# FF1 of a decoder layer: weight sums formed by accumulating transfers instead of VectorE

## The chip, the cores and the metric

The kernel runs on one core of a Trainium2 chip. The metric is the time of one execution on the device, in microseconds (us); less is better. A profile is one execution with the profiler on, with the busy time and the waits of each engine: TensorE (PE: matmuls; PEld: its weight loads), VectorE (DVE), ScalarE (ACT), GpSimd (POOL) and SyncE (SP), and the 16 DMA engines. Only SP and POOL issue transfers in this kernel.

## The reference

One decoder layer on 512 tokens with 2048 features, in float32. The first half (attention beside a recurrence) is not touched. The second half is

```python
h = rms_norm(x, g_pre_mlp[l]) * (1.0 + sc2) + sh2
f = jnp.square(jax.nn.relu(h @ w_ff1[l])) @ w_ff2[l]
x = x + gt2 * rms_norm(f, g_post_mlp[l])
```

with `w_ff1` of 2048 x 8192 and `w_ff2` of 8192 x 2048. FF1 is `h @ w_ff1` with its squared ReLU, FF2 the product with `w_ff2`.

## The kernel before

**Two parts for one number.** Each float32 operand of a product is split into `hi` (rounded to float32r by a ScalarE Copy) and `lo` (the rest, a VectorE subtract). A product is three matmuls, hi x hi, hi x lo and lo x hi (`mmh`, L1131 to L1133).

**Seven products for eight.** FF1 multiplies 2 x 2 blocks with seven products in place of eight: sums of weight blocks times sums of token blocks. A unit of output is q, 0 to 31: 256 rows of the hidden layer, as two halves of 128. The weights of q lie in HBM as four groups g, each `wff1[q, g]` of 128 x 1024: four blocks R0, R1, R2, R3 of 256 columns, in this order (both halves of the features, both halves of the output). The products need R1, R2, R3 as they are and four sums:

- S0 = R0 + R1, S1 = R0 + R2 (one VectorE add of 512 columns, L1290, with R0 read twice),
- S2 = S0 + R2 (L1293),
- S3 = S2 + R3 (L1294).

**The list of groups, `GR`.** It holds 16 entries of kind "a" (two blocks of two groups, no sums; their products are kept in `P1`), then 48 of kind "b" (q below 12: five products, R1 and the sums are split) and 80 of kind "c" (seven products, everything is split). A product of a group takes two steps of 128 rows, three matmuls each, so a "b" group has 5 x 2 x 3 = 30 matmuls of 128 x 256 and a "c" group 7 x 2 x 3 = 42.

**One turn of the loop, for group s:** `group(s)` issues the matmuls; `raw_load(s + 3)` issues the load of a later group into the tile `fr` (three of them; 512 KB by one transfer on SP's queue); `open_banks(s + 2)` clears PSUM; `forms(s + 2)` makes the sums in the tile `fs` (two of them), and splits blocks and sums into `fh` and `fl` (two of each, 1792 columns: three blocks, then four sums). It does so in two steps: Copy (L1289) and subtract (L1295) of the blocks, Copy (L1296) and subtract (L1297) of the sums. After the last group of q, `pair_end` combines the seven products on VectorE in `X`, applies ReLU and square on ScalarE into `ust` (two of them), and POOL stores the result to `ud` in HBM, 512 KB for a "c" q, 128 and 256 KB for a "b" q. FF2 reads it back from there.

**What sets the order.** The code is written in this order, and the framework then orders each engine's instructions by a plan of its own in which an instruction may pass earlier ones that are not ready; that order is fixed when the kernel is built. On the chip each engine and each DMA queue runs its list in order and waits at an instruction whose inputs or buffer are not ready. The tiles of `fp` (left side of SBUF) live for all of FF1. Those of `fp2` (right side: `fs`, `X`, `ust`) take the room of `h` (`hst`, `Hf`), so they come into being two groups ahead of the first "b" group, when `t_forms` has read the last of `h`.

Of the kernel before, what the change touches and what calls it, by code (L numbers as in the profile page):

```python
# [7 lines left out]
F32 = mybir.dt.float32  # L8
F32R = mybir.dt.float32r
AF = mybir.ActivationFunctionType  # L10
OP = mybir.AluOpType
# [119 lines left out]
def hybrid_block_kernel(ctx: ExitStack, tc: tile.TileContext, xT, c, vec, wada, wst, win, wv0, wv1,  # L131
                        w1, w2, pe, wrg, wout, wff1, wff2, xN, out):
    nc = tc.nc
    V, A, T, G = nc.vector, nc.scalar, nc.tensor, nc.gpsimd

    def f(ap):
        return ap.bitcast(F32)
# [10 lines left out]
    def ps(tag):  # L148
        return psum.tile([128, 512], F32, name="ps_" + tag, tag=tag, bufs=NB[tag])
# [250 lines left out]
    for j in range(4):  # L400
# [3 lines left out]
        p = ps("pj")  # L404
# [736 lines left out]
    def relu2(q, m, x, sgn, t_):  # L1141
        A.activation(x, x, AF.Relu, scale=sgn)
        A.activation(t_, x, AF.Square)

    def alpha_end(q, p, pool, tg, nb):
        A.activation(P1[q], p[:, T1], AF.Copy)
        x = pool.tile([128, 256], F32, name="ax", tag=tg, bufs=nb)
        u = pool.tile([128, 256], F32, name="au", tag=tg, bufs=nb)
        V.tensor_add(x, p[:, T2], P1[q])
        relu2(q, 0, x, 1.0, u)  # L1150
        G.dma_start(ud[q][:, 0, T1], u)
# [59 lines left out]
    fp = fst.enter_context(tc.tile_pool(name="fp", bufs=1, reuse_waits="tile"))  # L1211
    P1 = {q: fp.tile([128, 256], F32, name=f"p1_{q}") for q in range(NA1 + NA2)}
    for q in range(NA1):
        alpha_end(q, pf[q], fp, "ax", 2)
    THx = fp.tile([128, 2, 8, 256], F32R, name="thx")
    TLt = fp.tile([128, 4, D], F32R, name="tlt")
    TH = {5: lambda j: AH[:, j, T2], 7: lambda j: AL[:, j, T2],
# [7 lines left out]
    def hq(tok, kh, hh, of=Hf):  # L1225
        c0 = 1024 * kh + 512 * hh
        return of[:, 2 * tok:2 * tok + 2, c0:c0 + 512]

    def t_forms():
        for hh in range(2):  # L1230
            h11, h12, h21, h22 = hq(0, 0, hh), hq(1, 0, hh), hq(0, 1, hh), hq(1, 1, hh)
            ks_ = slice(4 * hh, 4 * hh + 4)

            def part(v, lo, hi):
                lo = lo.rearrange("p c (k t) -> p c k t", k=4)
                v = v.rearrange("p c (k t) -> p c k t", k=4)
                hi = hi.rearrange("p k (c t) -> p c k t", c=2)
                A.activation(hi, v, AF.Copy)
                V.tensor_sub(lo, v, f(hi))
            V.tensor_sub(h11, h11, h12)  # L1240
            yield
            V.tensor_sub(h12, h22, h12)
            yield
            V.scalar_tensor_tensor(h22, h11, -1.0, h22, op0=OP.mult, op1=OP.subtract)
            yield
            V.scalar_tensor_tensor(h21, h21, -1.0, h22, op0=OP.mult, op1=OP.subtract)
            yield
            for v, a_, hi in ((h11, (0, 0), AH[:, ks_, T2]), (h12, (1, 0), AL[:, ks_, T2]),
                              (h22, (1, 1), THx[:, 0, ks_]), (h21, (0, 1), THx[:, 1, ks_])):
                part(v, hq(*a_, hh, TLt), hi)  # L1250
                yield

    GR = []
# [4 lines left out]
    RAW, FM, FP2 = {}, {}, {}  # L1258
    gst = ExitStack()

    def raw_load(s):
        if s >= len(GR):
            return
        kind, q, g = GR[s]
        R = fp.tile([128, 1024], F32, name="fr", tag="fr", bufs=3)
        if kind == "a":
            nc.sync.dma_start(R.rearrange("p (a b) -> p a b", a=2),
                              wff1[q, g:g + 2, :, 512:].rearrange("a p b -> p a b"))
        else:
            nc.sync.dma_start(R, wff1[q, g])  # L1270
        RAW[s] = R

    def forms(s):
        if s >= len(GR):
            return
        kind = GR[s][0]
        R = RAW.pop(s)
        hi = fp.tile([128, 1792], F32R, name="fh", tag="fh", bufs=2)
        lo = fp.tile([128, 1792], F32R, name="fl", tag="fl", bufs=2)
        FM[s] = hi, lo  # L1280
        if kind == "a":
            for c_ in (0, 512):
                sl = slice(c_, c_ + 512)
                A.activation(hi[:, sl], R[:, sl], AF.Copy)
                V.tensor_sub(lo[:, sl], R[:, sl], f(hi[:, sl]))
            return
        Sm = FP2["p"].tile([128, 1024], F32, name="fs", tag="fs", bufs=2)
        n = 256 if kind == "b" else 768
        A.activation(hi[:, :n], R[:, 256:256 + n], AF.Copy)  # L1289
        V.tensor_add(Sm[:, :512].rearrange("p (a b) -> p a b", a=2),  # L1290
                     R[:, 256:768].rearrange("p (a b) -> p a b", a=2),
                     R[:, None, :256].to_broadcast([128, 2, 256]))
        V.tensor_add(Sm[:, 512:768], Sm[:, :256], R[:, 512:768])  # L1293
        V.tensor_add(Sm[:, 768:], Sm[:, 512:768], R[:, 768:])  # L1294
        V.tensor_sub(lo[:, :n], R[:, 256:256 + n], f(hi[:, :n]))  # L1295
        A.activation(hi[:, 768:], Sm, AF.Copy)  # L1296
        V.tensor_sub(lo[:, 768:], Sm, f(hi[:, 768:]))  # L1297

    banks = ["S", "T", "S", "T", "pj", "pj", "pj", "O"]
    nb = [-1]  # L1300
# [1 line left out]
    def bank():  # L1302
        nb[0] += 1
        return ps(banks[nb[0] % len(banks)])
# [8 lines left out]
    def open_banks(s):  # L1313
        if s >= len(GR) or GR[s] in asked:
            return
        kind, q, g = GR[s]
        if g:
            return
        asked.add(GR[s])
        pl = PLACE[kind].values()  # L1320
        BK[kind, q] = [bank() for _ in range(1 + max(b for b, _ in pl))]
        for b, half in pl:
            if half:
                A.activation(BK[kind, q][b][:, T2], zz, AF.Copy)
# [3 lines left out]
    def group(s):  # L1328
        kind, q, g = GR[s]
        hi, lo = FM.pop(s)  # L1330
        pl = PLACE[kind]
        open_banks(s)
        if kind == "a":
            todo = [(1 + h_, 2 * (g + a_) + j_, 512 * a_ + 256 * h_ + 128 * j_)
                    for a_ in range(2) for h_ in range(2) for j_ in range(2)]
        else:
            todo = [(l, 2 * g + j_, 256 * SLOT[l] + 128 * j_) for l in ORDER[kind] for j_ in range(2)]
        for l, j, c0 in todo:
            b, half = pl[l]
            o = BK[kind, q][b][:, 256 * half:256 * half + 256]  # L1340
            first = (kind, q, b) not in opened
            opened.add((kind, q, b))
            mmh(o, hi[:, c0:c0 + 128], lo[:, c0:c0 + 128], b_of(l, j), first, j == 7)
# [33 lines left out]
        G.dma_start(ud[q][:, 1], u[:, 1])  # L1377

    tg_ = t_forms()
    for s in range(3):  # L1380
        raw_load(s)
    forms(0)
    forms(1)
    for s, (kind, q, g) in enumerate(GR):
        group(s)
        raw_load(s + 3)
        if s + 2 < len(GR) and GR[s + 2][0] != "a" and not FP2:
            for _ in tg_:
                pass
            hst.close()  # L1390
            FP2["p"] = gst.enter_context(tc.tile_pool(name="fp2", bufs=1, side="right", reuse_waits="tile"))
        open_banks(s + 2)
        forms(s + 2)
        if kind == "a":
            next(tg_, None)
            if s % 4 == 3:
                next(tg_, None)
            if g == 2:
                pair_end(q, kind)
        elif g == 3:  # L1400
            pair_end(q, kind)
# [66 lines left out]
    for h in range(2):  # L1468
        OB = {(fb, ch): bank() for fb in range(2) for ch in range(4)}
        last = NL if h else 0  # L1470
        for q in range(32 - last):
            for mb in range(2):
# [4 lines left out]
                if mb == 0:  # L1477
                    i = 32 * h + q
# [87 lines left out]
```

## Time and profile before

| | |
|---|---|
| median of 3 runs | 2250.09 us (2248.28 to 2250.98) |
| the profiled execution | 2245.18 us, of which 2243.5 us are its span |
| mean granted clock of PE | 0.986 |
| PE busy | 2161.5 us, 96% of the span |
| VectorE busy | 1590.0 us, 71% |
| ScalarE busy | 1144.2 us, 51% |
| matmuls of FF1's "a" groups | from about 898 us |
| of its "b" groups | from about 948 us |
| of its "c" groups | from about 1120 us, to 1518 us |
| FF2 | from 1523.59 us to the end |

The span runs from the first to the last recorded instruction; the profiled execution's own time has what lies around it as well. Predicted and measured times are compared with the median of runs without a profile. A line of the profile names line, engine and operation, and out <- in by the program's names.

### The profile page before, as it was taken

What the parts mean: (1) busy time and instruction counts of PE and PEld (TensorE: products, weight loads), DVE (VectorE), ACT (ScalarE), POOL (GpSimd) and SP (SyncE); (2) the same over time, 40 slices, a digit from 0 to 9 for tenths busy, and PEclk for the clock granted to TensorE, in tenths of its full rate; (3) what the DMA queues carried; (4) which work ended last, traced back from release to release, by engine and by line L of the source; (5) the groups of instructions that cost most, each with busy time, mean ns of one, the idle gap of its engine ahead of it and who ended that gap; (6) DMA issues with size and microseconds to landing.
All of it is one profiled execution on the core that took longest, in us unless ns stands there. A gap on an engine that the chain in (4) does not pass through costs nothing.

```text
span 2243.5 us, 33596 instructions
## 1 busy us (share of the span) xinstructions
PE 2161.5 (96%) x12317; PEld 1853.6 (83%) x12317; DVE 1590.0 (71%) x3260; ACT 1144.2 (51%) x2139; POOL 40.5 (2%) x81
## 2 busy tenths in 40 slices
PE   7997999999989988999999999998999999999998
PEld 3686878878867867999999999997888888888886
DVE  8977999878886768799988888876654334333333
ACT  4348889559983237655555555554323333333331
POOL 0000000000000000000000000000000000000000
PEclk9999999999999999999999999999999999999999
DMA  9755545741238885655544434437877444444433
GB/s 378 309 219 157 177 157 170 242 148 59 72 103 273 286 266 167 192 171 177 178 131 138 135 123 134 139 133 258 300 244 229 141 144 146 143 143 146 143 122 113
DMA packets 138982, 398.41 MB, mean 178 GB/s; under 512 B 18609, under 2 KB 19777, under 8 KB 134465
## 3 DMA queue, kind: packets, MB, share of 16 engines
q1 hardware_dynamic: 132546, 375.31, 51.5%
q0 software_dynamic: 6272, 20.98, 2.5%
q8 instruction: 96, 1.57, 0.3%
q14 instruction: 68, 0.56, 0.1%
HBM read 366.84 MB, written 29.38 MB: 177 GB/s over the span
## 4 chain that ended last, share of the span: by engine, by line
PE 66%; issue 24%; DVE 5%; ACT 3%; DMA 1%; POOL 0%; DVEq 0%; SPq 0%; POOLq 0%; ACTq 0%
PE ps_pj L1445 4%; PE ps_pj L1444 4%; PE ps_pj L1446 4%; PE ps_pj L1131 3%; PE ps_pj L1132 3%; PE ps_pj L1133 3%; PE ps_T L1446 3%; PE ps_T L1444 3%; PE ps_S L1445 3%; PE ps_S L1444 3%; PE ps_S L1446 3%; PE ps_T L1445 3%; PE ps_T L1131 2%; PE ps_T L1133 2%; PE ps_T L1132 2%
## 5 line engine op out<-in xcount | busy, mean ns | idle before, releaser
L102 ACT ACTIVATE sl<-wr 128x512 fp32r<-128x512 f32 (+2 forms) x388 | 228.9, 613 | 342.4 <-DMA wr<-wout 91.4
L103 DVE TENSOR_TENSOR sl<-wr,sl 128x512 fp32r<-128x512 f32 (+2 forms) x388 | 256.1, 671 | 188.2 <-ACT sl L102 173.8
L218 DVE SCALAR_TENSOR_TENSOR md<-md,ca 128x512 f32<-128x512 f32 x256 | 170.2, 686 | 59.2 <-DMA md<-wada 38.4
L1289 ACT ACTIVATE fh<-fr 128x768 fp32r<-128x768 f32 (+1 forms) x128 | 87.3, 682 | 227.7 <-PE ps_T L1132 89.6
L177 PE MATMUL ps_pj<-AH,sl 128*128 128x512 f32 x384 | 161.7, 421 | 0.0
L1297 DVE TENSOR_TENSOR fl<-fs,fh 128x1024 fp32r<-128x1024 f32 x128 | 156.4, 1222 | 3.7 <-ACT fh L1296 3.6
L103 DVE TENSOR_TENSOR AL<-wr,AH 128x512 fp32r<-128x512 f32 x120 | 81.7, 689 | 108.6 <-ACT AH L102 108.6
L102 ACT ACTIVATE AH<-wr 128x512 fp32r<-128x512 f32 x120 | 73.5, 626 | 164.2 <-PE ps_O L1446 68.4
L178 PE MATMUL ps_pj<-AL,sl 128*128 128x512 f32 x384 | 153.2, 399 | 0.0
L179 PE MATMUL ps_pj<-AH,sl 128*128 128x512 f32 x384 | 153.0, 398 | 0.0
L1437 DVE TENSOR_TENSOR AL<-ur,AH 128x1024 fp32r<-128x1024 f32 x64 | 78.4, 1224 | 103.9 <-ACT AH L1436 103.6
L1295 DVE TENSOR_TENSOR fl<-fr,fh 128x768 fp32r<-128x768 f32 (+1 forms) x128 | 96.5, 754 | 53.2 <-ACT fh L1289 53.1
L1296 ACT ACTIVATE fh<-fs 128x1024 fp32r<-128x1024 f32 x128 | 133.6, 1044 | 0.0
L1436 ACT ACTIVATE AH<-ur 128x1024 fp32r<-128x1024 f32 x64 | 67.7, 1058 | 83.7 <-PE ps_T L1445 79.6
L1132 PE MATMUL ps_pj<-tlt,fh 128*128 128x256 f32 x368 | 103.7, 282 | 0.0
L1131 PE MATMUL ps_pj<-AH,fh 128*128 128x256 f32 x352 | 99.1, 282 | 0.0
L1133 PE MATMUL ps_pj<-AH,fl 128*128 128x256 f32 x352 | 98.4, 280 | 0.0
L1290 DVE TENSOR_TENSOR fs<-fr 128x512 f32<-128x512 f32 x128 | 88.2, 689 | 5.2 <-DMA fr<-wff 2.1
L1444 PE MATMUL ps_pj<-sl,AH 128*128 128x512 f32 x204 | 81.4, 399 | 5.5 <-ACT sl L102 5.5
L179 PEld LDWEIGHTS ps_pj<-AH,sl 128*128 128x128 f32 x384 | 72.5, 189 | 16.3 <-DVE sl L103 0.6
L177 PEld LDWEIGHTS ps_pj<-AH,sl 128*128 128x128 f32 x384 | 72.8, 190 | 11.7 <-ACT tr L818 0.6
L1445 PE MATMUL ps_pj<-sl,AH 128*128 128x512 f32 x204 | 81.4, 399 | 0.5 <-DVE sl L103 0.5
(567 smaller groups left out, 6821.7 us busy)
## 6 DMA issues: line engine op xcount, KB each, us to landing
fr<-wff SPq DMA_DIRECT2D x144, 512.0 KB, 3.6
md<-wada SPq DMA_DIRECT2D x256, 256.0 KB, 4.9
wr<-wff SPq DMA_DIRECT2D x128, 512.0 KB, 3.8
ur<-ud SPq DMA_DIRECT2D x64, 512.0 KB, 3.4
wr<-win SPq DMA_DIRECT2D x48, 512.0 KB, 3.4
ada<-wada SPq DMA_DIRECT2D x22, 1024.0 KB, 10.3
wr<-wout SPq DMA_DIRECT2D x36, 512.0 KB, 4.7
ud<-ust POOLq DMA_DIRECT2D x20, 512.0 KB, 3.0
```

The lines of the kernel that those rows point to most:

```text
L102: self.nc.scalar.activation(hi, raw, AF.Copy)
L103: self.nc.vector.tensor_sub(lo, raw, self.f(hi))
L177: T.matmul(o, wh, mh, start=start, stop=False)
L179: T.matmul(o, wl, mh, start=False, stop=stop)
L218: (V.scalar_tensor_tensor(w, w, 0.5, CA[0], op0=OP.mult, op1=OP.mult, accum_out=dq[s_][:, q_, k:k + 1]))
L1131: T.matmul(o, wh, b[0], start=start, stop=False, skip_group_check=True)
L1132: T.matmul(o, wh, b[1], start=False, stop=False, skip_group_check=True)
L1133: T.matmul(o, wl, b[0], start=False, stop=stop, skip_group_check=True)
L1297: V.tensor_sub(lo[:, 768:], Sm, f(hi[:, 768:]))
L1444: T.matmul(p, AH[:, k, hs], w[0], start=start, stop=False)
L1445: T.matmul(p, AH[:, k, hs], w[1], start=False, stop=False)
L1446: T.matmul(p, AL[:, k, hs], w[0], start=False, stop=stop)
```

## The change

It does four things.

- A "b" or "c" group gets one tile `fs` of 128 x 1792 (four of them, in `fp2`): R1, R2, R3, then S0 and S1, then S2 and S3. Its load is three transfers on SP's queue: R0 into the place of S0, R0 again into the place of S1, and R1 to R3. A fourth, on POOL's queue, reads R1 and R2 once more from HBM and adds them onto the two copies of R0 (`accum_op=OP.add`). It must wait for the first two.
- The first add of VectorE goes. S2 and S3 are made as before, in the tile itself.
- In a "c" group one Copy and one subtract of 1792 columns split everything; in a "b" group there are two pairs as before, of 256 and 1024 columns.
- The three `fr` tiles, now for "a" groups alone, move to a pool `frp` of their own, which is closed with `hst`, before `fp2` is opened. The loads of the first two "b" groups are issued at that point in the code, no longer ahead of it.

```diff
--- before.py
+++ after.py
@@ -1212,6 +1212,7 @@
     P1 = {q: fp.tile([128, 256], F32, name=f"p1_{q}") for q in range(NA1 + NA2)}
     for q in range(NA1):
         alpha_end(q, pf[q], fp, "ax", 2)
+    frs = ExitStack()
     THx = fp.tile([128, 2, 8, 256], F32R, name="thx")
     TLt = fp.tile([128, 4, D], F32R, name="tlt")
     TH = {5: lambda j: AH[:, j, T2], 7: lambda j: AL[:, j, T2],
@@ -1259,22 +1260,29 @@
     gst = ExitStack()
 
     def raw_load(s):
-        if s >= len(GR):
+        if s >= len(GR) or s in RAW:
             return
         kind, q, g = GR[s]
-        R = fp.tile([128, 1024], F32, name="fr", tag="fr", bufs=3)
         if kind == "a":
+            R = frp.tile([128, 1024], F32, name="fr", tag="fr", bufs=3)
             nc.sync.dma_start(R.rearrange("p (a b) -> p a b", a=2),
                               wff1[q, g:g + 2, :, 512:].rearrange("a p b -> p a b"))
+        elif FP2:
+            R = FP2["p"].tile([128, 1792], F32, name="fs", tag="fs", bufs=4)
+            two = R[:, 768:1280]
+            nc.sync.dma_start(two[:, :256], wff1[q, g, :, :256])
+            nc.sync.dma_start(two[:, 256:], wff1[q, g, :, :256])
+            nc.sync.dma_start(R[:, :768], wff1[q, g, :, 256:])
+            G.dma_start(two, wff1[q, g, :, 256:768], accum_op=OP.add)
         else:
-            nc.sync.dma_start(R, wff1[q, g])
+            return
         RAW[s] = R
 
     def forms(s):
         if s >= len(GR):
             return
         kind = GR[s][0]
-        R = RAW.pop(s)
+        R = RAW[s]
         hi = fp.tile([128, 1792], F32R, name="fh", tag="fh", bufs=2)
         lo = fp.tile([128, 1792], F32R, name="fl", tag="fl", bufs=2)
         FM[s] = hi, lo
@@ -1284,17 +1292,11 @@
                 A.activation(hi[:, sl], R[:, sl], AF.Copy)
                 V.tensor_sub(lo[:, sl], R[:, sl], f(hi[:, sl]))
             return
-        Sm = FP2["p"].tile([128, 1024], F32, name="fs", tag="fs", bufs=2)
-        n = 256 if kind == "b" else 768
-        A.activation(hi[:, :n], R[:, 256:256 + n], AF.Copy)
-        V.tensor_add(Sm[:, :512].rearrange("p (a b) -> p a b", a=2),
-                     R[:, 256:768].rearrange("p (a b) -> p a b", a=2),
-                     R[:, None, :256].to_broadcast([128, 2, 256]))
-        V.tensor_add(Sm[:, 512:768], Sm[:, :256], R[:, 512:768])
-        V.tensor_add(Sm[:, 768:], Sm[:, 512:768], R[:, 768:])
-        V.tensor_sub(lo[:, :n], R[:, 256:256 + n], f(hi[:, :n]))
-        A.activation(hi[:, 768:], Sm, AF.Copy)
-        V.tensor_sub(lo[:, 768:], Sm, f(hi[:, 768:]))
+        V.tensor_add(R[:, 1280:1536], R[:, 768:1024], R[:, 256:512])
+        V.tensor_add(R[:, 1536:1792], R[:, 1280:1536], R[:, 512:768])
+        for sl in (slice(0, 1792),) if kind == "c" else (slice(0, 256), slice(768, 1792)):
+            A.activation(hi[:, sl], R[:, sl], AF.Copy)
+            V.tensor_sub(lo[:, sl], R[:, sl], f(hi[:, sl]))
 
     banks = ["S", "T", "S", "T", "pj", "pj", "pj", "O"]
     nb = [-1]
@@ -1377,6 +1379,7 @@
         G.dma_start(ud[q][:, 1], u[:, 1])
 
     tg_ = t_forms()
+    frp = frs.enter_context(tc.tile_pool(name="frp", bufs=1, reuse_waits="tile"))
     for s in range(3):
         raw_load(s)
     forms(0)
@@ -1388,7 +1391,10 @@
             for _ in tg_:
                 pass
             hst.close()
+            frs.close()
             FP2["p"] = gst.enter_context(tc.tile_pool(name="fp2", bufs=1, side="right", reuse_waits="tile"))
+            for i in range(s + 2, s + 4):
+                raw_load(i)
         open_banks(s + 2)
         forms(s + 2)
         if kind == "a":
```

## Rows read from the trace of the kernel before

**Rows 1.** The page, busy us of each engine, share of the span, instructions.

```profile
PE 2161.5 (96%) x12317; PEld 1853.6 (83%) x12317; DVE 1590.0 (71%) x3260; ACT 1144.2 (51%) x2139; POOL 40.5 (2%) x81
```

**Rows 2.** Busy us by stretch: PE, PEld, DVE, ACT, POOL; clock, DMA share, GB/s.

```profile
...
0.00:56.00 56.00, 39.22 (x104) 20.43 (x105) 49.29 (x132) 23.83 (x43) 0.94 (x7) 0.91 0.97 377
...
1150.00:1490.00 340.00, 340.00 (x2873) 340.00 (x2873) 287.33 (x410) 182.03 (x257) 9.04 (x17) 1.00 0.42 133
960.00:1110.00 150.00, 150.00 (x1266) 150.00 (x1265) 143.83 (x255) 81.09 (x139) 10.71 (x20) 1.00 0.56 176
...
1530.00:1560.00 30.00, 30.00 (x131) 24.31 (x130) 20.31 (x43) 11.74 (x19) 0.00 (x0) 1.00 0.90 300
```

**Rows 3.** Waits, 960 to 1490 us: waiter, releaser; us, times, longest.

```profile
...
ACT fh L1289 <- PE ps_T L1132: 87.0, 35, 3.2
...
```

**Rows 4.** Groups by shape, 1150 to 1490 us: VectorE, then ScalarE.

```profile
...
L1297 DVE TENSOR_TENSOR fl<-fs,fh 128x1024 fp32r<-128x1024 f32 x68 | 83.1, 1223 | 0.0
L1295 DVE TENSOR_TENSOR fl<-fr,fh 128x768 fp32r<-128x768 f32 x69 | 65.9, 956 | 45.5 <-ACT fh L1289 45.5
L1290 DVE TENSOR_TENSOR fs<-fr 128x512 f32<-128x512 f32 x68 | 46.9, 689 | 1.9 <-DMA fr<-wff 0.2
L1294 DVE TENSOR_TENSOR fs<-fs,fr 128x256 f32<-128x256 f32 x69 | 29.3, 425 | 2.4
...
L1296 ACT ACTIVATE fh<-fs 128x1024 fp32r<-128x1024 f32 x69 | 72.0, 1044 | 0.0
L1289 ACT ACTIVATE fh<-fr 128x768 fp32r<-128x768 f32 x69 | 58.1, 841 | 141.5 <-PE ps_T L1132 73.7 <-PE ps_O L1132 67.8
```

**Rows 5.** Timeline of VectorE and ScalarE, one b group (start, us).

```profile
...
1044.53 0.69 DVE L1290 TENSOR_TENSOR fs<-fr 128x512 f32<-128x512 f32 x1
...
1046.06 0.42 DVE L1295 TENSOR_TENSOR fl<-fr,fh 128x256 fp32r<-128x256 f32 x1
1046.83 1.23 DVE L1297 TENSOR_TENSOR fl<-fs,fh 128x1024 fp32r<-128x1024 f32 x1 [0.35 <-ACT fh L1296]
...
1045.43 0.42 ACT L1289 ACTIVATE fh<-fr 128x256 fp32r<-128x256 f32 x1 [2.19 <-PE ps_pj L1132]
...
```

**Rows 6.** DMA queues, 1150 to 1490 us: packets, MB, share of 16 engines.

```profile
...
q1 hardware_dynamic: 9845, 35.81, 35.1%
q0 software_dynamic: 2448, 8.91, 6.6%
...
```

**Rows 7.** Instructions of two lines, duration in ns as min/median/max.

```profile
...
L1270 SPq DMA_DIRECT2D fr<-wff x128: 327/328/340, 938.8 to 1495.1; - x128
...
L1376 POOL DMA_DIRECT2D ud<-ust x12: 539/539/542, 970.1 to 1126.1; - x12
...
```

**Rows 8.** DMA issues of the whole span: KB each, median us to landing.

```profile
...
fr<-wff SPq DMA_DIRECT2D x144, 512.0 KB, 3.6
...
wr<-wrg SPq DMA_DIRECT2D x8, 128.0 KB, 2.2
...
ud<-ust POOLq DMA_DIRECT2D x12, 256.0 KB, 2.6
```

**Rows 9.** Timeline of SyncE and VectorE, the first b group.

```profile
...
938.75 23.11 SPq L1270 DMA_DIRECT2D fr<-wff  x8
...
940.68 1.29 DVE L1285 TENSOR_TENSOR fl<-fr,fh 128x512 fp32r<-128x512 f32 x2 [1.62 <-ACT fh L1284]
943.61 0.69 DVE L1290 TENSOR_TENSOR fs<-fr 128x512 f32<-128x512 f32 x1 [1.63 <-DMA fr<-wff]
...
945.14 1.29 DVE L1285 TENSOR_TENSOR fl<-fr,fh 128x512 fp32r<-128x512 f32 x2
...
948.80 1.23 DVE L1297 TENSOR_TENSOR fl<-fs,fh 128x1024 fp32r<-128x1024 f32 x1
...
```

**Rows 10.** Timeline of PE and ScalarE where FF2 begins.

```profile
...
1523.59 0.80 PE L1444 MATMUL ps_pj<-sl,AH 128*128 128x512 f32 x1 [5.46 <-ACT sl L102]
...
1521.98 1.04 ACT L1436 ACTIVATE AH<-ur 128x1024 fp32r<-128x1024 f32 x1
...
```

## The prediction

> **What bounds the kernel now.** I read the page's engine shares first, then the busy time by stretch, then the waits, and last the rows of the changed lines. The page gives PE as the engine that is nearly always busy [rows 1], but a share over the whole span says nothing of FF1, so the stretches decide. In the stretch of "b" groups (960 to 1110 us) and in that of "c" groups (1150 to 1490 us) PE is busy for all of 150.00 and all of 340.00 us at a granted clock of 1.00 [rows 2]. VectorE, which the change relieves, is busy 143.83 of 150 us beside the "b" groups: close to a bound, but PE does not wait for it. The waits of the same time say it the other way round: ScalarE's first split waits for PE to give a buffer back, 35 times for 87.0 us on one bank alone [rows 3]. So FF1 is paced by matmuls, which this change does not touch.
>
> The pace: 2873 matmuls in 340 us are 118.3 ns each, 1266 in 150 us are 118.5. A "c" group has 42 matmuls, so 4.97 us; a "b" group has 30, so 3.55 us. There are 80 and 48 of them.
>
> **What the change takes away.** For a "c" group VectorE now runs 0.69 + 0.43 + 0.43 (adds) + 0.96 + 1.22 (subtracts) = 3.73 us [rows 4]. The first add goes. The subtracts become one of 1792 columns; from the two rows it costs (1223 - 956)/256 = 1.04 ns a column, so 2.02 us. New sum 2.87 us: 0.86 us freed. ScalarE's 0.84 + 1.04 become one Copy of about 1.65 us. In a "b" group only the 0.69 us add goes, of 3.2 us in all [rows 5]. All of this lies under PE, so it is worth nothing. The new split takes 1.65 + 2.02 = 3.67 us from the release of the buffer to the last remainder, inside 4.97 us, so joining the halves should not make PE wait either.
>
> **What it adds, first: bytes.** Now a group loads 512 KiB. After, it loads 128 + 128 + 384 KiB plainly and 256 KiB that are added onto what lies in SBUF. The accumulating kind is nowhere in this trace. Its price lies between one plain transfer of its bytes and three (source read, old value read, sum written); I take two: a plain transfer is a read and a write and is priced as one, and the accumulation has one read more. The stores of a "b" group add 384 KiB per four groups, 96 KiB. In all, 736 KiB = 753.7 kB plain, and 262.1, 524.3 or 786.4 kB for the accumulation.
>
> How fast can it go? The busiest long stretches move 300 GB/s at a DMA share of 0.90, so 333 GB/s at a full share, and 377 at 0.97, so 389 [rows 2]. I use 333, where the loads have the size of these. The group then needs 3.05 us at price one, 3.84 us at two and 4.62 us at three, against 3.55. At two, each of the 48 "b" groups is 0.284 us too slow: 13.6 us. A "c" group has 128 KiB of stores; at three it needs 1572.9/333 = 4.72 us, still under 4.97. So the "c" stage is covered up to three, the "b" stage is not.
>
> A rule to weigh here: the shares of the two queues add up, 35.1% for SP's and 6.6% for POOL's make almost all of the 0.42 [rows 2, 6]. The Trainium skill (DMA: Bandwidth & Descriptors, "Issuing engines are not separate DMA queues") says that transfers issued from different engines run on the same 16 DMA engines and interleave, and these shares agree. If POOL's accumulations had lanes of their own, 753.7 kB would need 2.26 us and the price would be nothing; on shared lanes it is the 3.84 us above. The Trainium skill (Collectives: The Full Stack, Part 3, on the bandwidth ceiling) also says that a sum inside a DMA runs at half rate because it reads two sources; no run here shows it, and by it the sum would again be 3.84 us.
>
> **Second: a longer way from free tile to sum.** A tile is released by its group's last subtract, 0.42 + 1.04 + 1.22 = 2.68 us after a "b" group's split starts [rows 4, 5]. Then come two issues on SP at 0.33 [rows 7], the landing of a 128 KiB load (2.2 us, the nearest row [rows 8]), POOL's issue at 0.54 [rows 7], the accumulation, and two adds, 0.84. A 256 KiB store from POOL lands in 2.6 us, a 512 KiB load in 3.6 [rows 8]; I take 3.6, with 2.6 and 5 as ends. That makes 10.5 us. Four tiles give 4 x 3.55 = 14.2 us for it ("c": 11.5 of 19.9). So the latency is covered, with 3.7 us of lead, which is eaten before the shortage of 0.284 us a group reaches PE: 13.6 - 3.7 = 9.9 us.
>
> What is queued: SP issues three loads a group, 1.0 of 3.55 us, with nothing else behind them until FF2's first loads. POOL's accumulation waits for two loads, and the stores of u wait behind it; these have two buffers and are read only in FF2, so nobody waits for them. The reverse matters more: an accumulation queued behind a store waits for a whole pair's end.
>
> **Third: the first "b" group.** Today its load is issued at 938.75 us, before the last "a" groups are split, and its first add waits for it until 943.61 [rows 9]. After, its tile lies in the room of frp and of the old h, and fr tiles are read until 941.97 (second last "a" group) or 946.43 (last). From the issue, 0.33 + 2.2 + 0.54 + 3.6 + 0.84 + 1.04 + 1.22 = 9.8 us pass to the last remainder, which today ends at 950.03. Issued at 938.75 that costs nothing; behind the second last group 1.7 us; behind the last 6.2 us. A tile of 7 KiB covers at least part of two fr tiles of 4 KiB, so I take the middle case, 2.0 us.
>
> **Sum.** 9.9 + 2.0 = 11.9 us. The profiled execution took 2245.2 us (span 2243.5), so it would become 2257.1. The median of the runs is 2250.1, 4.9 us above the profiled one; on it I predict 2262.0 us.
>
> **Rivals.** A difference under 0.2%, 4.5 us here, can't be told from none.
>
> *Hidden after all (not slower).* If an accumulation costs like a plain transfer, or the engines reach the 389 GB/s of the kernel's start, a "b" group needs 3.05 to 3.29 us and fits; only the start is left, 0 to 6.2 us: 2250 to 2256, mostly 2252. It decides at 1183 kB a group, an accumulation priced at 1.6 (at 333). For it: the share is only 0.56 today. Against it: it leaves nothing for rows of 1 KiB in place of 4.
>
> *VectorE waits in its queue.* Adds now wait for a DMA in front of other work. If the order on VectorE puts a tile's adds ahead of a subtract of an earlier group, that subtract waits for the accumulation, its tile is freed late, and the next accumulation with it: a ring of two "c" groups of 0.66 + 2.2 + 0.54 + L + 0.85 + 2.02 = 6.3 + L against 9.94. Beyond L = 3.7 us each of 80 groups loses half the excess: at 4.5 us 33 us, at 5 us 53 us. With the forecast's 11.9 that is 2295 to 2315. Against it: today a group's adds stand directly before its own subtracts [rows 5].
>
> *The accumulation is far dearer than three.* Then "c" groups are bound too, and each further 262 kB costs 0.79 us in 128 groups, 101 us: 2350 and up.
>
> *Faster.* FF2's first matmul starts after 5.46 us of idle time; ScalarE comes to FF2's first split at 1521.98, behind the last pair's end, though the last matmul of FF1 is over at about 1518.1 [rows 10]. A new order on ScalarE could win up to 3.9 us there: 2246, and below 2245.6 only with something more. I see nothing in the change that asks for it.
>
> **Chances.** The forecast (the "b" stage paced by transfers) 0.38, alone 2255 to 2285; hidden 0.28, of which 0.23 stay within 0.2%; VectorE's queue 0.20; a far dearer accumulation 0.07; faster 0.07, of which 0.03 within 0.2%. Slower: 0.38 + 0.05 + 0.20 + 0.07 = 0.70; same 0.26; faster 0.04. The range 2249 to 2325 leaves out the far dearer accumulation, the faster case and the ends of two others, about 0.2.
>
> **What the profile after would show.** Right: PE idle only in the "b" stretch, about 0.2 us a group, a DMA share there near 1, PE at 100% in the "c" stretch; a gap of some 2 us more than now before the first "b" group; VectorE down by about 0.86 us a "c" group and no time won by it. Wrong: PE at 100% in both stretches (hidden), subtracts that start late behind adds which wait for a DMA (VectorE's queue), or accumulations that land after more than 5 us in the "c" stretch.

## The result, and the profile of the changed kernel

The changed kernel takes 2428.56 us (median, 2427.49 to 2434.16) against 2249.21 us before, a ratio of 1.0801 (95% interval 1.0783 to 1.0820). It is slower by 179 us, where 12 were forecast, and lies outside the range. The profiled execution has a span of 2427.4 us.

The engines' row of the changed kernel's page:

```profile
PE 2223.3 (92%) x12317; PEld 1896.7 (78%) x12317; DVE 1493.2 (62%) x3052; ACT 1142.1 (47%) x2059; POOL 152.8 (6%) x209
```

Its busy time by stretch (PE, PEld, DVE, ACT, POOL; then clock, DMA share, GB/s):

```profile
960.00:1110.00 150.00, 123.65 (x917) 118.37 (x918) 88.17 (x154) 58.54 (x97) 34.12 (x44) 0.93 0.82 206
1230.00:1660.00 430.00, 365.53 (x2861) 356.50 (x2861) 226.54 (x272) 176.50 (x188) 68.00 (x85) 0.96 0.65 168
```

The two stretches lie in the "b" and in the "c" groups. PE was never idle in either [rows 2]; now it is idle for 26 of 150 and 64 of 430 us. Neither VectorE nor the DMA engines are full in its place: the DMA share is 0.65 where the larger loss is. So something waits in a circle. The waits of FF1 name it (waiter, releaser; us, times, longest):

```profile
DVE fs L1295 <- DMA fs<-wff: 289.6, 98, 6.9
POOL fs L1276 <- DMA fs<-wff: 260.1, 67, 8.5
ACT fh L1298 <- PE ps_O L1132: 85.9, 27, 7.4
...
PEld ps_pj L1133 <- DVE fl L1299: 65.1, 37, 5.6
PE ps_pj L1133 <- DVE fl L1299: 57.4, 36, 5.4
```

VectorE's first add (L1295) stands still for 290 us in all until an accumulation lands; PE then waits for VectorE's subtract (L1299). Before, the first add of a group sat idle for 1.9 us in 340 [rows 4]. The groups by shape, 1230 to 1660 us (count, busy us and mean ns, idle before it and its releaser):

```profile
L1299 DVE TENSOR_TENSOR fl<-fs,fh 128x1792 fp32r<-128x1792 f32 x68 | 137.3, 2019 | 17.1 <-ACT fh L1298 16.2 <-DMA fs<-wff 0.8
L1276 POOL DMA_DIRECT2D fs<-wff x68 | 58.4, 859 | 296.1 <-DMA fs<-wff 167.0 <-DVE fs L1296 54.7 <-DVE fl L1299 23.9
...
L1295 DVE TENSOR_TENSOR fs<-fs 128x256 f32<-128x256 f32 x68 | 28.9, 425 | 182.8 <-DMA fs<-wff 182.7
L1296 DVE TENSOR_TENSOR fs<-fs 128x256 f32<-128x256 f32 x68 | 28.8, 423 | 1.7
```

The durations are as forecast: 2.02 us for the joined subtract, 0.43 for an add. What is new is the idle time ahead of the add, 2.7 us a group. One round of the circle, in the timeline of VectorE, then of SyncE, GpSimd and ScalarE (start us, us, instruction, idle before it):

```profile
1401.51 2.02 DVE L1299 TENSOR_TENSOR fl<-fs,fh 128x1792 fp32r<-128x1792 f32 x1
1406.04 0.42 DVE L1295 TENSOR_TENSOR fs<-fs 128x256 f32<-128x256 f32 x1 [2.52 <-DMA fs<-wff]
1406.38 0.68 DVE L1362 TENSOR_TENSOR X<-ps_T,X 128x512 f32<-128x512 f32 x1
...
1407.32 0.68 DVE L1366 TENSOR_TENSOR X<-ps_S,X 128x512 f32<-128x512 f32 x1
1408.10 0.69 DVE L1367 TENSOR_TENSOR X<-ps_T,X 128x512 f32<-128x512 f32 x1
1408.71 2.02 DVE L1299 TENSOR_TENSOR fl<-fs,fh 128x1792 fp32r<-128x1792 f32 x1
...
1411.88 0.42 DVE L1295 TENSOR_TENSOR fs<-fs 128x256 f32<-128x256 f32 x1 [0.82 <-DMA fs<-wff]
1412.34 0.43 DVE L1296 TENSOR_TENSOR fs<-fs 128x256 f32<-128x256 f32 x1
1414.44 2.03 DVE L1299 TENSOR_TENSOR fl<-fs,fh 128x1792 fp32r<-128x1792 f32 x1 [1.68 <-ACT fh L1298]
...
1403.55 0.33 SPq L1273 DMA_DIRECT2D fs<-wff  x1
...
1416.50 0.33 SPq L1273 DMA_DIRECT2D fs<-wff  x1
...
1407.70 0.86 POOL L1276 DMA_DIRECT2D fs<-wff  x1 [4.56 <-DVE fs L1296]
...
1412.73 1.68 ACT L1298 ACTIVATE fh<-fs 128x1792 fp32r<-128x1792 f32 x1
```

Number the groups so that the subtract that ends at 1403.53 is that of group s. It frees the tile of group s + 4: SP issues that tile's loads at 1403.55, POOL its accumulation at 1407.70 (the plain loads had to land; the name in brackets is only what ended last beside them), and the sum is there at 1411.88, where VectorE's add of group s + 4 waits for it. Only behind this add stands the subtract of group s + 2, 1414.44 to 1416.47; it frees the tile of group s + 6, whose loads are issued at 1416.50. So two groups take 12.95 us here, where PE needs 9.94. (The subtract at 1408.71 and the loads at 1410.76, not shown, are those of the round that runs one group behind.)

The order of instructions on VectorE shows why. "+82" are the adds of group 82, "-80" is the last subtract of group 80, other work left out:

```
before                 -79 +81 -80 +82 -81 +83 -82
changed kernel ("c")   -79 +82 -80 +83 -81 +84 -82
changed kernel ("b")   -19 +21 -20 +22 -21 +23 -22 +24 -22 -23   (+24 stands between the two subtracts of 22)
```

Before, the sums had two tiles, so the adds of group 82 wrote where the subtract of group 80 still read: they could not be put ahead of it. With four tiles the fixed order that the framework writes puts them one group further ahead in the "c" groups. In the "b" groups it stays close to the order of before (-20 +22 -21 there too); only one add in four goes further. What is new in both stages is that an add which stands ahead of an earlier group's subtract now waits for an accumulation.

Stage times, from PE's rows of each profiled execution (the "b" groups from their first matmul to the first of the "c" groups, the "c" groups to the end of their last). The last column sums, over the first "b" group, every step of more than 0.3 us from the start of one matmul to the start of the next, less the usual 0.118; it comes out up to 0.8 us above the idle time in the profile's brackets, which counts from a matmul's end:

| kernel | "b" groups | "c" groups | stop of PE at first "b" group |
|---|---|---|---|
| before | 171.5 | 398.0 | 0.6 |
| changed kernel | 248.6 | 502.1 | 8.6 |
| e_order | 198.7 | 400.1 | 9.0 |
| e_plain | 223.2 | 458.9 | 7.8 |
| e_order_plain | 185.7 | 400.1 | 7.7 |
| e_order_early | 196.7 | 400.2 | 5.6 |
| e_five | 255.6 | 518.8 | 9.7 |
| e_store | 255.0 | 524.7 | 9.1 |
| e_split | 190.0 | 400.3 | 5.0 |
| e_split_order | 177.4 | 398.3 | 4.5 |
| e_c_only | 176.6 | 398.7 | 3.0 |

Of the changed kernel's loss 104 us lie in the "c" groups and 77 in the "b" groups; the "a" groups (49.0 against 50.3) and the edge to FF2 (5.45 us of idle time against 5.46 [rows 10]) are as before.

### The profile page after: what moved, and what is told of

Its sections match the earlier page's. It is cut to its first block, busy times and chain, and to the rows that moved or that the text cites. A ratio compares the mean times of both kernels' runs of the same rounds, so it can differ in the third digit from the quotient of the medians.

```text
span 2427.4 us, 34169 instructions
## 1 busy us (share of the span) xinstructions
PE 2223.3 (92%) x12317; PEld 1896.7 (78%) x12317; DVE 1493.2 (62%) x3052; ACT 1142.1 (47%) x2059; POOL 152.8 (6%) x209
## 4 chain that ended last, share of the span: by engine, by line
PE 39%; issue 25%; DMA 19%; DVE 12%; ACT 4%; SPq 1%; POOL 0%; DVEq 0%; POOLq 0%; ACTq 0%
DMA fs<-wff 18%; DVE fl L1299 4%; PE ps_pj L1451 4%; PE ps_pj L1452 4%; PE ps_pj L1450 4%; PE ps_T L1452 2%; PE ps_T L1450 2%; PE ps_S L1451 2%; PE ps_S L1450 2%; PE ps_S L1452 2%; PE ps_T L1451 2%; PE ps_O L1452 1%; PE ps_O L1450 1%; PE ps_O L1451 1%; ACT fh L1298 1%
## 5 line engine op out<-in xcount | busy, mean ns | idle before, releaser
L1298 ACT ACTIVATE fh<-fs 128x1792 fp32r<-128x1792 f32 (+2 forms) x176 | 202.4, 1170 | 273.8 <-PE ps_O L1132 85.9
L1299 DVE TENSOR_TENSOR fl<-fs,fh 128x1792 fp32r<-128x1792 f32 (+2 forms) x176 | 238.3, 1365 | 49.8 <-ACT fh L1298 46.8
L1295 DVE TENSOR_TENSOR fs<-fs 128x256 f32<-128x256 f32 x128 | 54.3, 424 | 289.7 <-DMA fs<-wff 289.6
L1133 PE MATMUL ps_pj<-AH,fl 128*128 128x256 f32 x352 | 106.2, 302 | 50.9 <-DVE fl L1299 50.9
L1276 POOL DMA_DIRECT2D fs<-wff x128 | 110.9, 866 | 493.7 <-DMA fs<-wff 260.1
L1133 PEld LDWEIGHTS ps_pj<-AH,fl 128*128 128x128 f32 x352 | 70.3, 200 | 57.5 <-DVE fl L1299 57.5
L1133 PE MATMUL ps_S<-AH,fl 128*128 128x256 f32 x248 | 76.0, 306 | 42.5 <-DVE fl L1299 41.4
L1133 PEld LDWEIGHTS ps_S<-AH,fl 128*128 128x128 f32 x248 | 49.5, 199 | 49.6 <-DVE fl L1299 47.7
L179 PEld LDWEIGHTS ps_pj<-AH,sl 128*128 128x128 f32 x384 | 72.7, 189 | 17.6 <-DVE sl L103 1.7
L1450 PE MATMUL ps_pj<-sl,AH 128*128 128x512 f32 x204 | 81.4, 399 | 5.5 <-ACT sl L102 5.5
```

Source lines behind the costliest of these rows:

```text
L179: T.matmul(o, wl, mh, start=False, stop=stop)
L1133: T.matmul(o, wl, b[0], start=False, stop=stop, skip_group_check=True)
L1450: T.matmul(p, AH[:, k, hs], w[0], start=start, stop=False)
```

## The experiments

The theory after the result: VectorE's order makes the ring. Rivals: the accumulation itself is too dear; four tiles are too few; the bytes fill the DMA engines; accumulations are held up behind stores on POOL's queue.

### e_order: the adds of a tile behind the last subtract of the tile before

```diff
+        with tc.issue_after(LAST[0].ins):
-        V.tensor_add(R[:, 1280:1536], R[:, 768:1024], R[:, 256:512])
+            V.tensor_add(R[:, 1280:1536], R[:, 768:1024], R[:, 256:512])
...
-            V.tensor_sub(lo[:, sl], R[:, sl], f(hi[:, sl]))
+            LAST[0] = V.tensor_sub(lo[:, sl], R[:, sl], f(hi[:, sl]))
```

> Changed kernel, with one edit: on VectorE the adds of a tile are kept behind the last subtract of the tile before it (today the adds of tile s + 2 stand before the subtract of tile s in the c stage). Nothing else differs, the transfers are the same. Theory 1, a ring through VectorE's queue (subtract, loads, accumulation, adds, next subtract but one): the ring then spans four groups and no longer sets the pace; the c stage goes back from 502 us to about 400, the b stage from 249 to about 200 (there the DMA engines were busy 0.80 of 5.18 us a group, 4.1 us, more than the 3.57 of before); in all about 2285 us. Theory 2, the transfers themselves are the bound: no change, 2420 to 2435 us.

Measured: 2281.41 us, 1.0150 of before (1.0128 to 1.0173). The order is now -79 +80 -80 +81 -81: each add stands two groups later than in the changed kernel's "c" groups, and one group later than in the kernel before. No transfer, tile or instruction differs from the changed kernel, and 147 of its 179 us are gone. The framework plans the other engines' orders anew with the edit: in the "c" groups, past the first few, all that moves is one ReLU of each pair's end on ScalarE; in the "b" groups ScalarE's, GpSimd's and PE's orders differ in places too. The busy time by stretch ("b", then "c"):

```profile
960.00:1130.00 170.00, 160.34 (x1278) 155.61 (x1279) 117.14 (x214) 85.47 (x137) 48.78 (x63) 0.98 0.97 251
1180.00:1540.00 360.00, 360.00 (x3042) 360.00 (x3042) 242.12 (x289) 181.53 (x196) 72.33 (x91) 1.00 0.85 215
```

In the "c" groups PE is busy throughout, though more bytes a second are moved (215 against 168 GB/s): the ring was the order. In the "b" groups the DMA share is now 0.97, and PE is short of work by 9.7 us of 170 with matmuls at a slightly lower clock: this is the shortage that was forecast.

### e_plain and e_order_plain: a plain transfer in place of the accumulation

```diff
-            G.dma_start(two, wff1[q, g, :, 256:768], accum_op=OP.add)
+            G.dma_start(two, wff1[q, g, :, 256:768])
```

Both leave R0 out of the two sums that the accumulation makes. e_plain is the changed kernel with this edit alone, e_order_plain has the order of e_order as well.

> Changed kernel, POOL's accumulating transfer replaced by a plain one of the same bytes to the same place (so R0 is left out of the two sums and the output differs from the reference's); VectorE's order is the same as in the changed kernel. Theory 1, the ring: it gets shorter only by what a plain transfer lands sooner (about 1.5 us of some 12 to 12.5 for two groups), so the c stage falls to 440 to 460 us and the whole to 2330 to 2360. Theory 2, the accumulating kind is too dear for the DMA engines: with it gone the loss is gone but for the start, 2255 to 2265 us.

> VectorE's adds behind the subtract of the tile before, and POOL's transfer plain in place of accumulating (so R0 is left out of two sums). With the accumulating transfer and this order the b stage took 198.7 us at a DMA share of 0.97. If the accumulating kind is what fills the DMA engines: the share in the b stage falls to about 0.8 and the stage to 172 to 180 us, in all 2255 to 2265 us. If it is the additional bytes and the shorter rows whatever the kind: the b stage stays at 190 us or more, in all 2272 us or more.

Measured: e_plain 2363.39 us, 1.0509 (1.0483 to 1.0534); e_order_plain 2266.55 us, 1.0088 (1.0073 to 1.0103). With a transfer of the plain kind the ring is shorter, the "c" groups take 458.9 us as expected (the whole 3 us more than expected), but it is still there: the kind of transfer is worth 65 us in the changed order and 15 in the order of e_order, and the order is worth 147 us with the accumulation and 97 without. So a dear accumulation alone doesn't explain the result. e_order_plain came out between its two expectations: the DMA share in the "b" stretch falls to about 0.8 as the first says, but the "b" groups still take 185.7 us.

The two orders are a measurement of the accumulation's price too. DMA queues and issues of e_order, 960 to 1130 us (packets, MB, share of 16 engines; KB each, median us to landing):

```profile
q1 hardware_dynamic: 18151, 27.55, 50.8%
q0 software_dynamic: 7401, 14.97, 46.1%
...
fs<-wff POOLq DMA_DIRECT2D x43, 256.0 KB, 5.7
fs<-wff SPq DMA_DIRECT2D x86, 128.0 KB, 4.5
ud<-ust POOLq DMA_DIRECT2D x10, 256.0 KB, 5.4
```

and the queues of e_order_plain in the same stretch:

```profile
q1 hardware_dynamic: 19872, 30.16, 54.5%
q0 software_dynamic: 4934, 15.93, 28.3%
```

A MB on SP's queue takes the same share in both, 1.84 and 1.81 points. On POOL's queue a plain MB takes 28.3/15.93 = 1.78. In e_order ten pairs of stores, 3.93 MB, take 7.0 of 46.1 points at that price; the other 39.1 go to 43 accumulations, 11.27 MB: 3.47 points a MB, about 1.95 times the plain price.

### e_five: a fifth tile

```diff
-            R = FP2["p"].tile([128, 1792], F32, name="fs", tag="fs", bufs=4)
+            R = FP2["p"].tile([128, 1792], F32, name="fs", tag="fs", bufs=5)
...
-        raw_load(s + 3)
+        raw_load(s + 4 if FP2 else s + 3)
```

One tile `ust` in place of two makes the room.

> Changed kernel with five tiles fs in place of four (paid for with one tile ust in place of two), the loads issued one group earlier. VectorE's order then has the adds of tile s + 3 before the subtract of tile s, so the ring through it is as short as before. Theory 1, the ring: the c stage stays at 490 to 510 us, the whole within 20 us of 2428. Theory 3, too few tiles for the longer way from a free tile to its sum: a fifth more tiles give a fifth more time, the c stage falls to about 405 us, the whole below 2330.

Measured: 2455.54 us, 1.0919 (1.0882 to 1.0955), 27 us slower than the changed kernel, a little outside what the ring theory allowed. The written order moved with the tiles: -79 +83 -80 +84 -81, the adds now three ahead, so a ring still holds two groups. A fifth tile did not help while the order followed the tiles. The edit also issues the loads a group earlier and takes one `ust` away; which of the three costs the 27 us stays open.

### e_store: the stores of u on ScalarE's queue

```diff
-            G.dma_start(ud[q], u)
+            A.dma_start(ud[q], u)
```

(and the same for the two stores of a "b" unit)

> The changed kernel with the stores of u issued from ScalarE's queue in place of POOL's, so that no accumulation is queued behind a store that waits for the end of a pair. In the changed kernel POOL waited some 71 us for ust between 950 and 1690 us. Order on VectorE: in the stretch of c groups the order of adds and subtracts is that of the changed kernel, the adds of a tile ahead of the subtract of the tile two before. If that order makes the ring, the stretch of c groups stays at 490 to 510 us and the time at 2410 to 2435 us. If accumulations held back behind stores on POOL's queue make the stall, the stretch falls by most of the 71 us, to 450 or less, and the time to 2370 us or less.

Measured: 2459.86 us, 1.0935 (1.0874 to 1.0997), "c" groups 524.7 us. No gain: accumulations behind stores were not what held the "c" groups. It came out 25 us above what the theory gave: VectorE's first add waits 320.0 us for accumulations, where it waited 289.6 in the changed kernel; why stays open. The changed kernel's trace agrees that POOL's queue is not the cause: in its "c" groups an accumulation is issued 0.56 us (median) after the second load of R0 lands.

### e_split and e_split_order: one Copy and one subtract, no accumulation

The rest of the change by itself. R0 is loaded once into a tile of 2048 columns, and VectorE makes all sums:

```diff
+            R = FP2["p"].tile([128, 2048], F32, name="fs", tag="fs", bufs=4)
+            nc.sync.dma_start(R[:, 1792:], wff1[q, g, :, :256])
...
-            G.dma_start(two, wff1[q, g, :, 256:768], accum_op=OP.add)
...
+        V.tensor_add(R[:, 768:1280].rearrange("p (a b) -> p a b", a=2),
+                     R[:, :512].rearrange("p (a b) -> p a b", a=2),
+                     R[:, None, 1792:].to_broadcast([128, 2, 256]))
```

e_split_order also puts these adds behind the last subtract of the tile before the last, as they stood before the change.

> Changed kernel without accumulation: R0 is loaded once, plainly, beside R1 to R3 in a tile of 2048 columns, and VectorE makes all four sums again; the one Copy and one subtract a group, the four tiles, frp and the late loads of the first b groups stay, and VectorE's order is again two tiles ahead. Theory 1: with a plain load the ring takes about 8 us for two groups, under 9.9, so only the late start is left: 2252 to 2260 us. A theory in which the joined split (one Copy, one subtract of 1792 columns) holds PE up: 2270 us and more.

> The kernel without accumulation (four tiles, one Copy and one subtract a group, plain loads), with the adds of a tile kept behind the last subtract of the tile before the last, as they stand in the kernel before. Without this its b stage took 190.0 us against 171.5. Theory 1, the ring through VectorE's queue: in the b stage its adds stood two tiles ahead too, and two b groups are 7.1 us where the ring with a plain load takes some 8; with the order back the b stage takes 171 to 174 us and only the start is left, 2252 to 2258 us. A theory in which the joined split or the layout of the tile costs the 18 us: 2270 us as without the order.

Measured: e_split 2271.61 us, 1.0099 (1.0080 to 1.0118), a miss; e_split_order 2253.90 us, 1.0027 (1.0015 to 1.0038), as expected. The miss teaches most. e_split has no accumulation, and yet in the "c" groups its order is that of the changed kernel, -79 +82 -80 +83, and in the "b" groups it goes further than there, +22 -20 +23 -21: with four tiles the adds go two ahead. The "c" groups hardly mind (400.3 us), but the "b" groups lose 18.5 us. The first add of e_split in the groups by line, 960 to 1130 us, then the busy time in that stretch of e_split, and of e_split_order:

```profile
L1292 DVE TENSOR_TENSOR fs<-fs 128x512 f32<-128x512 f32 x45 | 30.9, 687 | 22.2 <-DMA fs<-wff 22.2
```

```profile
960.00:1130.00 170.00, 159.51 (x1285) 155.19 (x1286) 144.28 (x262) 82.24 (x141) 11.24 (x21) 0.99 0.52 161
```

```profile
960.00:1130.00 170.00, 170.00 (x1433) 169.81 (x1433) 158.57 (x280) 90.19 (x150) 11.82 (x22) 1.00 0.53 172
```

The add waits 22 us for plain loads, at a DMA share of 0.52, and PE is short of work; once the order is put back, PE is busy throughout. So joining Copy and subtract in the "c" groups costs PE nothing, as forecast (398.3 against 398.0 us), and the order alone makes a ring even of plain loads when groups are short.

### e_order_early: tiles that are free sooner

```diff
+            FP2["p"].tile([128, 7, 256], F32, name="X", tag="X", bufs=1)
+            FP2["p"].tile([128, 2, S], F32, name="ust", tag="ust", bufs=2)
```

Opened ahead of the first `fs`, these two take the room that `fr` still uses.

> The kernel with VectorE's adds behind the subtract of the tile before, accumulating, with X and ust placed under the tiles fs, so that no fs tile lies where an fr tile is still read. In the run without this the first b group started 9.0 us late. If its loads wait for the room of fr: they are issued about 5 us earlier, and PE's idle time at the first b group falls to 2 to 5 us, in all 2274 to 2278 us. If the wait is for something else (the accumulation itself, POOL's store ahead of it): no change, 2281 us.

Measured: 2278.15 us, 1.0142 (1.0123 to 1.0161), at the edge of what was expected. The 3 us to e_order are not clear of the noise (the two intervals overlap), but in the traces PE's stop at the first "b" group falls from 9.0 to 5.6 us, no more. GpSimd's timeline shows the limit:

```profile
942.20 0.54 POOL L1151 DMA_DIRECT2D ud<-au  x1 [5.14 <-ACT au L1143]
948.93 0.54 POOL L1151 DMA_DIRECT2D ud<-au  x1 [6.18 <-DMA fs<-wff]
949.87 1.81 POOL L1276 DMA_DIRECT2D fs<-wff  x2 [0.39 <-DMA fs<-wff]
```

The first loads go out at 938.52 us in place of 946.80 in e_order, but the first accumulation only at 949.87 (951.66): it is queued on POOL behind a store of the "a" stage, which waits for `au`, the result that it stores.

### e_c_only: accumulation in the "c" groups alone

e_order_early's tiles and order in the "c" groups, and in the "b" groups the sums of e_split_order:

```diff
+            if kind == "c":
+                G.dma_start(two, wff1[q, g, :, 256:768], accum_op=OP.add)
...
+        with tc.issue_after((PREV[-2] if kind == "b" else LAST[0]).ins):
```

> Accumulation in the c groups alone; the b groups load R0 plainly and VectorE makes their sums, in the order of the kernel before; c adds behind the subtract of the tile before; X and ust placed under fs. If the loss of the run with the right order is the b stage's transfers (0.97 share there, 0.85 in the c stage) and the start: both are gone, FF1 takes what it took before, 2247 to 2254 us, within 0.2% of the kernel before. If the accumulation costs PE something in the c stage too: 2256 us or more.

Measured: 2252.88 us, 1.0023 (1.0013 to 1.0034) of before on the same chip, inside the expected 2247 to 2254 us. The stretches "b" and "c", and the ten us behind the first "b" group's wait:

```profile
960.00:1130.00 170.00, 170.00 (x1432) 169.71 (x1430) 155.27 (x275) 92.17 (x153) 15.36 (x26) 1.00 0.57 179
1230.00:1490.00 260.00, 260.00 (x2198) 260.00 (x2198) 173.78 (x208) 132.28 (x144) 52.02 (x65) 1.00 0.83 211
...
954.00:964.00 10.00, 10.00 (x70) 10.00 (x69) 6.99 (x13) 2.73 (x4) 0.00 (x0) 0.78 0.42 141
```

PE is busy throughout both stages. With the accumulation only where transfers have room and the order pinned, the change costs what is lost at and just behind the first "b" group, some 5 us, and gains nothing: VectorE's busy time in the "c" groups falls to 174 of 260 us (287 of 340 before [rows 2]), and PE had not waited for it. No version beat the kernel before. No run has the accumulation in the "c" groups with the order of the kernel before, so it stays open whether that order would have been enough there.

## Why the prediction was wrong, point by point

- **What bounds FF1** was right: PE. All freed time of VectorE and ScalarE was worth nothing (e_c_only, e_split_order).
- **The step that failed** is the overlap in "Second": "Four tiles give 4 x 3.55 = 14.2 us for it ("c": 11.5 of 19.9). So the latency is covered". The way from a free tile to its sum was given four groups' time. In the changed kernel's "c" groups it has two: the adds of group s + 4 stand on VectorE ahead of the subtract of group s + 2, so that subtract waits for the accumulation, and two groups take 12.55 us (502.1/80 = 6.28 each) where PE needs 9.94. The sum had nothing for this. e_order shows it: with the adds behind the subtracts, 147 us go.
- **The prediction knew this as a rival**, "VectorE waits in its queue", at a chance of 0.20, and the argument against it was a misreading: "today a group's adds stand directly before its own subtracts [rows 5]". The adds in those rows belong to the next group. The Copy of the sums whose remainder is taken at 1046.83 starts before the last add shown ends:

```profile
1045.72 0.42 DVE L1294 TENSOR_TENSOR fs<-fs,fr 128x256 f32<-128x256 f32 x1
...
1045.75 1.04 ACT L1296 ACTIVATE fh<-fs 128x1024 fp32r<-128x1024 f32 x1
```

So in the kernel before, in "b" and "c" groups alike, the adds already stood one group ahead (-20 +22 -21, -80 +82 -81), and the pair of tiles was what kept them from going further; the change took that limit away.

- **The price of that rival** was too low as well: 2295 to 2315. Its ring was 6.3 us + L for two "c" groups, 9.9 us at L = 3.6, so at the prediction's own L it had no slack against 9.94. The accumulation was sized well: 0.54 + 3.6 = 4.14 us from POOL's issue to the landing; the median measured is 4.1, counted from the start of the issue, so that the 0.86 us of the issue lie within it. What was too short is the plain load, 2.2 us where 3.5 is the median in the "c" stretch, with 0.56 more until POOL issues; with these medians the ring is 11.4 us. Two terms were left out. In the round shown, 1.68 us pass while the subtract waits for ScalarE's Copy (16.2 us over the 68 groups of the stretch). And at a pair's end, in every fourth group, VectorE's adds into `X` stand between an add and the subtract behind it: 2.67 us from 1406.04 to 1408.71, where 0.8 is the median. In the "b" groups, at which that rival put nothing, the order is worth 50 us (248.6 against 198.7): two groups take 7.1 us of PE there, so a ring is too long sooner.

The landings, from the DMA issues of the changed kernel, 1300 to 1660 us (KB each, median us to landing):

```profile
fs<-wff SPq DMA_DIRECT2D x57, 384.0 KB, 4.3
fs<-wff SPq DMA_DIRECT2D x115, 128.0 KB, 3.5
fs<-wff POOLq DMA_DIRECT2D x57, 256.0 KB, 4.1
ud<-ust POOLq DMA_DIRECT2D x14, 512.0 KB, 3.9
```

- **The idle time is not all of it.** In the "c" groups PE stands for 80 of the 104 us lost, by the measure of the table's last column (71 by the profile's idle time). The other 24 are matmuls that start 0.20 to 0.24 us apart, twice the 0.118 of before: behind the stops PE runs for a while at the lower level of its clock (the granted clock is 0.96 in the stretch above). The prediction did not have this term.
- **The accumulation's price** was right: two plain transfers taken, 1.95 measured. The Trainium skill (Collectives: The Full Stack, Part 3, on the bandwidth ceiling) says of a collective's ReduceScatter that it runs at half the rate of a copy because the add needs two source reads; the 1.95 measured here, for a transfer on one core, agrees.
- **The shortage in the "b" groups** was right in its mechanism and close in its rate: 3.84 us a group forecast; e_order takes (198.7 - 9.0)/48 = 3.95 us a group behind its late start, at a DMA share of 0.97. What was wrong is the lead of 3.7 us that was taken off: the tiles start late, not early. So the stage loses 27 us (198.7 against 171.5), 9 of them at the start, in place of 9.9 + 2.0. e_c_only, without accumulations there, loses 5.
- **The first "b" group** was forecast at 2.0 us, with 6.2 as the far end; PE waits 8.16. The tile came free as in the middle case, behind the second last "a" group. But the accumulation stood on POOL behind a store of `au` (for some 1 us: its second load had landed at 948.69), and, the larger part, it landed after 8.3 us, beside the loads of three further tiles, where 3.6 was taken. Timeline of the changed kernel:

```profile
945.31 0.34 SPq L1273 DMA_DIRECT2D fs<-wff  x1
...
949.23 0.54 POOL L1151 DMA_DIRECT2D ud<-au  x1 [4.97 <-ACT au L1143]
950.17 0.91 POOL L1276 DMA_DIRECT2D fs<-wff  x1 [0.40 <-DMA fs<-wff]
958.52 0.43 DVE L1295 TENSOR_TENSOR fs<-fs 128x256 f32<-128x256 f32 x1 [6.14 <-DMA fs<-wff]
960.55 0.58 PE L1131 MATMUL ps_T<-AH,fh 128*128 128x256 f32 x1 [8.16 <-ACT fh L1298]
```

- **Adding up:** of the 179 us the order explains 147 (e_order against the changed kernel), what the accumulation brings to the "b" groups most of the rest (e_order against e_c_only, 2281.41 and 2252.88, 28 us, of which some 3 by the earlier tiles), and the start of the "b" stage the last 5. The shares hold for this sequence alone (with plain transfers the order is worth 97). From e_order_early to e_c_only the loads and the order of the "b" groups change together; the kind of transfer alone is worth 15 (e_order against e_order_plain). Why the plain e_order_plain still takes 185.7 us in the "b" groups, 9 more than e_c_only, stays open: it has two transfers more a group and its adds a group later.

## What to carry to other kernels

A tile with few buffers also limits an order: before giving a value more buffers, look at which instruction the old count kept from moving ahead. Read from the tiles which group an instruction belongs to, not from where it stands: neighbours in a queue can be of different groups. An instruction that waits for a DMA must not stand on an in-order engine ahead of the instruction that frees that DMA's buffer one or two rounds on; pin it behind. And take landings of a transfer from a stretch with as many transfers in flight as there will be.

## What the runs showed of the hardware

- An accumulating transfer of 256 KiB from HBM onto SBUF takes 1.95 times the DMA engines' time of a plain one, 0.86 us of POOL's time to issue against 0.55, and lands in 4.1 to 5.7 us from the start of its issue (medians, at DMA shares from 0.65 to 0.97), the longer the fuller the engines.
- A short wait of PE costs more than itself: in e_c_only PE waits 1.59 and 0.80 us in the first "b" group, and in the stretch behind it, 954 to 964 us, the granted clock is 0.78, a mean of its levels of 1.2 and 2.4 GHz; 70 matmuls run there where 87 ran in the same stretch of the kernel before.
